# Attention's V projection made ahead of the scores: two tiles plainly, six in three pairs by Strassen's algorithm

## The chip, the cores and the metric

The kernel runs on one core of a Trainium2 chip. The metric is the device time of one execution in microseconds (us), lower is better. A core has a matrix engine (TensorE, PE in the profile), VectorE (DVE), ScalarE (ACT), GpSimd (POOL), a queue engine (SyncE, SP) and 16 DMA engines. Each engine works through its own instructions in the order in which the program has them, and waits on semaphores for the others. Matrix products are written to PSUM; the other tiles lie in SBUF. Only DVE, ACT and PE reach PSUM.

## The reference

Two pre-normed residual layers on x of 1024 x 1024, in float32. Layer one is a gated DeltaNet followed by a convolutional FFN, layer two is a banded softmax attention followed by another FFN. What the change touches is the way from the first FFN into attention:

```python
h = h + conv_ffn(rmsnorm(h, f_norm[0]), f_w_up[0], f_conv[0], f_conv_b[0], f_w_down[0])
kv = rmsnorm(h, kv_norm) @ w_kv            # K: columns 0..1023, V: columns 1024..2047
q = rmsnorm(h, b_norm) @ b_w_q
# for each of 16 heads of 64 and each chunk of 64 queries, a band of 9 chunks of keys
s = q_chunk @ k_band.T * 64 ** -0.5 + bias
o_chunk = softmax(s) @ v_band
h = h + o @ b_w_out
```

## The kernel before

**Numbers.** Every dense product in float32 is done as three products of reduced type: an operand is split into a high part (a cast on ACT, `xh`, `whi`, `uh`) and a low part (the difference, on POOL or DVE, `xl`, `wlo`, `ul`), and high x high, low x high and high x low are added up in one PSUM tile. Lines 118 to 120 hold the three matmuls of a plain tile (function `dense`), lines 1446 to 1448 those of the FFN.

**FFN 0.** Its up and down products go by Strassen's algorithm, with sums of weight blocks made by DVE, split by ACT and POOL (`r`, then `uh` and `ul`); the last tile of hidden columns is done plainly (`pul`, then the down products `pf`, with weights `fr` split into `fh` and `fl`). Everything around the end of the FFN stands in an order written out by hand: a list of steps for TensorE, and jobs hung at a step with a rank. SP issues the weight loads, POOL the accumulating stores `d_r<-stage`.

**Norm.** `norm_steps` (line 346 on) squares and sums h, and then makes, for each of the 8 row blocks k and for the half s of 512 tokens, `nt` (DVE), `xh` (ACT) and `xl` (line 381). With k even `xl` is made by DVE, with k odd by POOL.

**K0 and Q0.** `two_tiles` (line 1385) makes the K and the Q of the first pair of heads: first halves of both, with the rest of the norm's second half put in between, then second halves. Behind the second half of K0 the weights of V0 are loaded, folded with the norm's gain (line 98) and split (lines 101, 103).

**Attention.** There are 8 pairs of heads p. For each pair the kernel makes K, Q and V tiles of 128 columns, each in two halves of 8 x 3 matmuls (24 a half, 48 a tile). K and Q go through ACT and DVE (`kA`, `qA`, `qL`); V has to stand with tokens on partitions. For p = 0 that is done by transposes on TensorE (`pvt`); for p > 0 the tile is copied as 16-bit halves (`vt`), stored to DRAM (`d_vt`) and read back by a transposing DMA (`vu`), then joined (`vf`) and split into high and low (`V`). A score tile `sc` (lines 2293, 2294) is reduced and moved to `sS` by DVE (line 2298), raised by ACT (line 2302), divided by its sum by POOL (line 2308), transposed by TensorE (`ptp`, line 2353), split by ACT and DVE (`pTh`, `pTl`), and multiplied by V (`poT`, lines 2398, 2399), whose result ACT and DVE move to `oT`. There is one PSUM tile for `sc`.

**The order in attention** is made at build time by a planner (class `Flow`): it keeps an estimate of when DVE, ACT and POOL come free, emits score, transpose and apply groups when their inputs should be there, and otherwise matmuls of the next dense tile in its list `wv.dense`. That list holds for each pair K, Q and V (from p = 1 on; V from p = 0 on), in `queue_kv`. A K or Q tile may start when pair p - 2 is scored, a V tile when the outputs of pair p - 2 are done; their buffers come free then. After the last of them the tiles of the out-projection (`acco`) take their place.

Of the kernel before, what the change touches and what calls it, by code (L numbers as in the profile page):

```python
# [9 lines left out]
F32 = mybir.dt.float32  # L10
F32R = mybir.dt.float32r
# [7 lines left out]
KT = 8  # L19
# [9 lines left out]
def trunk_kernel(  # L29
# [1355 lines left out]
    def two_tiles(wts, tail, then):  # L1385

        pss = [[pacc.tile([P, HALF], F32, name="acc", tag="u", bufs=4) for _ in range(2)] for _ in wts]
        for s in range(2):
            for n, (ps, wt) in enumerate(zip(pss, wts)):
                for i in range(KT):  # L1390
                    dense(ps[s], wt, 0, xh, xl, FULL[i : i + 1], s, first=i == 0, last=i == KT - 1)
                    if (n, i) in ((0, 6), (1, 3)):
                        next(tail, None)
                if (s, n) == (1, 0):
                    then()
            for _ in tail:
                pass
            yield pss
# [8 lines left out]
    def ffn(layer, h, hp, xs, tail, d_r, last):  # L1407
# [475 lines left out]
        if layer == 0:  # L1883
# [187 lines left out]
        return right, norms[1] if norms else None  # L2071
# [8 lines left out]
    ctx_f, tail0 = ffn(0, h, hp, normed, tails[0], d_r0, xb)  # L2080
# [5 lines left out]
    def next_tile():  # L2086
        raw = wp.tile([P, KT, P], F32, name="wraw", tag="wraw", bufs=2)
        nc.sync.dma_start(out=raw, in_=w_kv[:, 1024 : 1024 + P].rearrange("(k p) m -> p k m", p=P))
        ready.append(split_w(raw, [P, KT, P], fold=g_kv))

    first = two_tiles([load_w(w_kv, 0, fold=g_kv, on_act=True), load_w(b_w_q, 0, fold=g_b, on_act=True)], tail0, next_tile)
    next(first)
# [4 lines left out]
    with ExitStack() as ph:  # L2097
# [21 lines left out]
        def kv_tile(src, c0, g, post):  # L2119

            if ready:
                wt = ready.pop()
                yield
            else:
                shape = [P, KT, P]
                raw = wp.tile(shape, F32, name="wraw", tag="wraw", bufs=2)
                nc.sync.dma_start(out=raw, in_=src[:, c0 : c0 + P].rearrange("(k p) m -> p k m", p=P))
                yield
                wt = split_w(raw, shape, fold=g)
                wv.on("G", 3.61, wv.on("A", 0.89, wv.on("G", 2.6)))  # L2130
# [13 lines left out]
        def queue_kv(p):  # L2144
# [18 lines left out]
            def post_q(s, ps):  # L2163
# [7 lines left out]
                def low():  # L2171
# [5 lines left out]
                    if s == 1:  # L2177
                        wv.mark(("kq", p), t)
# [545 lines left out]
```

## Time and profile before

| | us |
|---|---|
| median of 3 runs | 2497.43 (2497.12 to 2500.88) |
| span of the profiled execution | 2493.3 |
| DeltaNet and FFN 0, to the first K and Q matmul | 1295 |
| K0, Q0 and V0, to the first score | 37 |
| attention, first to last score (1332.4 to 1760.3) | 428 |
| the rest of the out-projection and FFN 1 | 733 |

Times in a row are from the span's start. In a timeline row the first number is the start, the second the duration; "x3" joins three like instructions; what stands in brackets is the idle time of the engine before the row and the engine and operation that ended it. In the rows of groups the total busy time and the mean of one in nanoseconds come after the bar. A matmul's duration in such a row covers its way through a pipeline, so that one starts well before the one ahead of it ends; what one costs TensorE is the interval between two starts.

### The profile page before, as it was taken

How to read it: one execution, taken by the hardware profiler on the slowest of the kernel's cores; microseconds unless marked ns; L12 is line 12 of the kernel's file. 1: busy time of each engine (PE TensorE's matmuls, PEld its weight loads, DVE VectorE, ACT ScalarE, POOL GpSimd, SP SyncE). 2: the span in 40 equal slices, each digit the busy share in tenths (PEclk: the TensorE clock that was granted, in tenths of full speed). 3: DMA queues.
4: the chain of work that ended last, by engine and by line, in shares of the span. 5: the costliest groups of instructions: out<-in, count | busy, mean ns of one | idle time of the engine just before them, and what ended most of it. 6: DMA issues, size and time to landing. Idle time of an engine off the chain costs nothing.

```text
span 2493.3 us, 39279 instructions
## 1 busy us (share of the span) xinstructions
PE 2466.1 (99%) x13785; PEld 2057.0 (83%) x13785; DVE 1842.5 (74%) x2985; ACT 1442.1 (58%) x2770; POOL 1523.0 (61%) x1548
## 2 busy tenths in 40 slices
PE   8999999999999999999999999999999999999998
PEld 6888888888888888888788888888877888888877
DVE  5665874567798888888866656666589788888886
ACT  6444546474465556565555666667456565666555
POOL 3655653357357777777626454455554777778774
PEclk9999999999999999999999999999999999999999
DMA  8734435565347777777841232333444799777788
GB/s 228 188 105 118 142 110 153 156 194 163 96 108 148 150 153 151 153 144 156 183 151 55 67 80 77 81 76 95 145 114 119 184 176 180 166 169 171 152 187 224
DMA packets 383877, 353.19 MB, mean 142 GB/s; under 512 B 97600, under 2 KB 304448, under 8 KB 383680
## 3 DMA queue, kind: packets, MB, share of 16 engines
q1 hardware_dynamic: 350704, 243.46, 34.4%
q0 software_dynamic: 28224, 98.58, 22.5%
q10 hardware_dynamic: 4752, 8.65, 0.9%
q8 instruction: 108, 1.77, 0.3%
q14 instruction: 89, 0.73, 0.1%
HBM read 182.25 MB, written 156.30 MB: 136 GB/s over the span
## 4 chain that ended last, share of the span: by engine, by line
PE 81%; POOL 6%; DVE 4%; issue 4%; DMA 2%; ACT 2%; SPq 0%; ACTq 0%; POOLq 0%; DVEq 0%
PE acc L118 8%; PE pu L1448 8%; PE acc L119 8%; PE acc L120 8%; PE pu L1446 8%; PE pu L1447 8%; PE pd L1448 3%; PE pd L1446 3%; PE pd L1447 3%; POOL ul L1412 3%; PE acco L118 2%; PE acco L120 2%; PE acco L119 2%; PE ptp L2353 2%; PE poT L2399 1%
## 5 line engine op out<-in xcount | busy, mean ns | idle before, releaser
L1412 POOL TENSOR_TENSOR ul<-r,uh 128x512 fp32r<-128x512 f32 x266 | 430.4, 1638 | 258.3 <-ACT uh L1434 253.5
L118 PE MATMUL acc<-xh,whi 128*128 128x512 f32 x896 | 369.3, 413 | 0.5 <-ACT xh L1094 0.5
L119 PE MATMUL acc<-xl,whi 128*128 128x512 f32 x896 | 352.1, 393 | 0.4 <-POOL xl L381 0.3
L120 PE MATMUL acc<-xh,wlo 128*128 128x512 f32 x896 | 351.3, 392 | 0.0
L103 POOL TENSOR_TENSOR wlo<-wraw,whi 128x256 fp32r<-128x256 f32 (+1 forms) x326 | 237.0, 758 | 107.8 <-ACT whi L101 105.3
L1434 ACT CAST uh<-r 128x512 fp32r<-128x512 f32 x289 | 177.1, 623 | 183.3 <-DVE r L1412 148.8
L1448 PE MATMUL pu<-xh,ul 128*128 128x512 f32 x524 | 204.4, 390 | 0.7 <-POOL ul L1412 0.7
L1446 PE MATMUL pu<-xh,uh 128*128 128x512 f32 x524 | 204.4, 390 | 0.7 <-ACT keep L1575 0.7
L1802 ACT COPY stage<-pd 128x1024 f32<-128x1024 f32 x180 | 175.3, 1014 | 49.7 <-PE pd L1448 48.8
L1447 PE MATMUL pu<-xl,uh 128*128 128x512 f32 x524 | 203.9, 389 | 0.0
L120 PEld LDWEIGHTS acc<-xh,wlo 128*128 128x128 f32 x896 | 168.5, 188 | 37.1
L2308 POOL TENSOR_SCALAR sS<-sS,st 128x640 f32<-128x640 f32 (+4 forms) x128 | 87.6, 691 | 178.4 <-DVE st L2306 168.2
L119 PEld LDWEIGHTS acc<-xl,whi 128*128 128x128 f32 x896 | 169.3, 189 | 28.4 <-POOL xl L381 2.5
L118 PEld LDWEIGHTS acc<-xh,whi 128*128 128x128 f32 x896 | 169.1, 189 | 27.5 <-ACT xh L1094 0.9
L1412 POOL TENSOR_TENSOR dl<-a,dh 128x512 fp32r<-128x512 f32 x90 | 153.3, 1703 | 47.4 <-ACT dh L1434 37.2
L1541 DVE SCALAR_TENSOR_TENSOR gate<-gpre,colt,gate 128x1023 f32<-128x1023 f32 (+2 forms) x92 | 176.5, 1919 | 2.5 <-ACT gate L1538 1.8
L1541 DVE SCALAR_TENSOR_TENSOR val<-vpre,colt,val 128x1023 f32<-128x1023 f32 x88 | 149.2, 1696 | 29.3 <-ACT val L1538 29.3
L2298 DVE CUSTOM_DVE_ANT_0 sS<-sc,bt 128x640 f32<-128x640 f32 (+4 forms) x128 | 84.1, 657 | 111.4 <-PE sc L2294 75.9
L1412 DVE TENSOR_TENSOR r<-r,r 128x512 f32<-128x512 f32 x160 | 130.3, 814 | 32.8 <-POOL ul L1412 31.7
L1412 DVE TENSOR_TENSOR el<-val,eh 128x512 fp32r<-128x512 f32 x90 | 85.4, 949 | 43.2 <-ACT eh L1434 43.2
L1448 PEld LDWEIGHTS pu<-xh,ul 128*128 128x128 f32 x524 | 98.4, 188 | 22.8 <-POOL ul L1412 1.4
L1446 PEld LDWEIGHTS pu<-xh,uh 128*128 128x128 f32 x524 | 98.4, 188 | 21.1 <-ACT keep L1575 1.1
(428 smaller groups left out, 7197.9 us busy)
## 6 DMA issues: line engine op xcount, KB each, us to landing
r<-in_f_w_up_dram SPq DMA_DIRECT2D x176, 256.0 KB, 4.5
d_r<-stage POOLq DMA_DIRECT2D x78, 512.0 KB, 8.1
d_c<-stage POOLq DMA_DIRECT2D x70, 512.0 KB, 8.4
a<-in_f_w_down_dram SPq DMA_DIRECT2D x72, 256.0 KB, 2.9
wraw<-in_a_w_in_dram SPq DMA_DIRECT2D x32, 512.0 KB, 4.5
d_e<-stage POOLq DMA_DIRECT2D x32, 512.0 KB, 8.3
wraw<-in_a_w_out_dram SPq DMA_DIRECT2D x16, 512.0 KB, 4.1
d_r<-h ACTq DMA_DIRECT2D x32, 256.0 KB, 2.8
```

The costliest lines, as they stand in the source:

```text
L103: nc.gpsimd.tensor_tensor(lo[:, c], raw[:, c], hi[:, c].bitcast(F32), op=ALU.subtract)
L118: mm(ps, hi[:, kw, wcol : wcol + P], rh[k][s], start=st, stop=False)
L119: mm(ps, hi[:, kw, wcol : wcol + P], rl[k][s], start=False, stop=False)
L120: mm(ps, lo[:, kw, wcol : wcol + P], rh[k][s], start=False, stop=sp)
L1412: tt = lambda eng, o, a, b, op: eng.tensor_tensor(o, a, b, op=op)
L1434: copy(hi, src)
L1446: mm(ps, w[0][:, cw], x[0], start=first, stop=False, skip_group_check=True)
L1447: mm(ps, w[0][:, cw], x[1], start=False, stop=False, skip_group_check=True)
L1448: mm(ps, w[1][:, cw], x[0], start=False, stop=last, skip_group_check=True)
L1541: nc.vector.scalar_tensor_tensor(t_[:, a:c1], p_[:, a - step : c1 - step], w[:, 2 - step : 3 - step], t_[:, a:c1], op0=ALU.mult, op1=ALU.add)
L1802: nc.scalar.copy(t_, ps)
L2308: nc.gpsimd.tensor_scalar(S, S, st[:, 3:4], 1.0, op0=ALU.mult, op1=ALU.mult)
```

## The change

- The eight V tiles are no longer made in attention. They are made between FFN 0 and the first score, in the pools of FFN 0, whose buffers stay open for that.
- V0 and V1 are made plainly: first halves in `first_halves`, which takes the place of `two_tiles` and carries the rest of the norm, second halves in the new `values`.
- V2 to V7 are made as three pairs. Pair j is a product of a weight block of 1024 x 256, taken as 2 x 2 blocks of 512 x 128 (`v11`, `v12`, `v21`, `v22`), with the normed activations as 2 x 2 blocks, by the seven products of Strassen's algorithm in Winograd's form. A product is 4 x 3 = 12 matmuls. Each needs a weight operand (a sum of blocks by DVE, `uh` by ACT, `ul` by POOL) and an activation operand (`X`: blocks of the norm's output, or sums that are made once for all three pairs and split).
- The raw weight blocks are loaded into buffers that FFN 0's last weights leave (tags `r11` to `r22` and the like), and folded with the gain on POOL.
- Every V half is copied to `vt` and stored to one of 16 `d_vt` tensors. In attention the transposing reads are all that is left of V; the `pvt` transposes go.
- Then K0 and Q0 are made in one go, just ahead of attention. `wv.dense` holds K and Q of pairs 1 to 7 only, 14 tiles in place of 22.
- The norm's second half is called with `keep=True`, which writes `nt` in place into h, and for which `norm_steps` has `xl` of k = 0..3 made by POOL and of k = 4..7 by DVE.

The core of the diff:

```diff
-    def two_tiles(wts, tail, then):
...
+    def first_halves(wts, tail):
+        pss = [pacc.tile([P, HALF], F32, name="acc", tag="u", bufs=4) for _ in wts]
+        for n, (ps, wt) in enumerate(zip(pss, wts)):
+            for i in range(KT):
+                dense(ps, wt, 0, xh, xl, FULL[i : i + 1], 0, first=i == 0, last=i == KT - 1)
+                if (n, i) in ((0, 6), (1, 3)):
+                    next(tail, None)
...
+    def values(wts, pss, raw, load, fh, fin, wf, wd, d_vt, more):
...
+        def lows(n, k):
+            tt(nc.gpsimd if k % 2 else nc.vector, X[n][k][1], place[n](k), X[n][k][0].bitcast(F32), sub)
+
+        def fold(j, q):
...
+            tt(nc.gpsimd, t_, t_, g, ALU.mult)
...
+        def operand(j, n):
+            left_sum(j, n)
+            src = raw[j, {1: 11, 2: 12, 7: 21, 6: 21, 5: 11, 4: 22, 3: 12}[n]]
+            hi, lo = ops[j, n] = [wf.tile([P, HALF], F32R, name="u" + x, tag="u" + x, bufs=3) for x in "hl"]
+            nc.scalar.copy(hi, src)
+            tt(nc.gpsimd, lo, src, hi.bitcast(F32), sub)
+
+        def product(j, n):
...
+            for k in range(4):
+                x_ = X[n][k]
+                mm(ps, wh[:, kc[k]], x_[0], start=o == n and k == 0, stop=False, skip_group_check=True)
+                mm(ps, wh[:, kc[k]], x_[1], start=False, stop=False, skip_group_check=True)
+                mm(ps, wl[:, kc[k]], x_[0], start=False, stop=k == 3, skip_group_check=True)
...
+        def out(tile_, s, src):
+            turn[0] ^= 1
+            vt = wf.tile([P, 2, 4, P], mybir.dt.uint16, name="vt", tag=("dh", "dl")[turn[0]], bufs=2)
+            nc.scalar.copy(vt.rearrange("p h b t -> p h (b t)"), src.bitcast(mybir.dt.uint16).rearrange("p (t h) -> p h t", h=2))
+            nc.sync.dma_start(out=d_vt[2 * tile_ + s].rearrange("(h b c) t -> c h b t", h=2, b=4), in_=vt)
...
+        plan = [(1, 1), (2, 1), (1, 2), (3, 1), (2, 2), (3, 2)] + [(j, n) for n in (7, 6) for j in range(1, 4)] + [(1, 5), (2, 5), (1, 3), (3, 5), (2, 3), (3, 3)] + [(j, 4) for j in range(1, 4)]
+        for j, n in plan:
+            step((j, n), lambda j=j, n=n: product(j, n))
+            at(pos[j, n] - 2, lambda j=j, n=n: operand(j, n), 1)
+            at(pos[j, n] + 1, lambda j=j, n=n: after(j, n), 0)
...
+        for j, i in ((1, -1), (2, 2), (3, 4)):
+            for q, d in ((11, 0), (12, 1), (21, 4), (22, 5)):
+                at(i + d, lambda j=j, q=q: fold(j, q), 0.5)
...
-                        norms.append(norm_steps(fh, s, None, last))
+                        norms.append(norm_steps(fh, s, None, last, keep=True))
...
-            for n, (src, c0, g, post) in enumerate(((w_kv, p * P, g_kv, post_k), (b_w_q, p * P, g_b, post_q), (w_kv, 1024 + p * P, g_kv, post_v))):
-                if p > 0 or n == 2:
-                    free = [] if p < 2 else [(("scored", "o")[n == 2], p - 2)]
-                    wv.dense.append((lambda: True, there(*free), kv_tile(src, c0, g, post)))
+            for src, g, post in ((w_kv, g_kv, post_k), (b_w_q, g_b, post_q)):
+                free = [] if p < 2 else [("scored", p - 2)]
+                wv.dense.append((lambda: True, there(*free), kv_tile(src, p * P, g, post)))
```

How the order of the instructions moves at three places. First POOL at the end of FFN 0, from the last but two `ul` of the last tile on. `fl` and `ul` are low parts of the down and up weights, `v11` and `v12` raw blocks of V's weights that are folded, and the `wlo` are the low parts of K0's and Q0's weights before, of V0's and V1's after. Before:

```order
L1412 TENSOR_TENSOR ul_12679<-r11_12494,uh_12678 128x512
L1412 TENSOR_TENSOR fl3_12708<-fr_12603,fh3_12707 128x512
L1412 TENSOR_TENSOR ul_12726<-r12_12608,uh_12725 128x512
L1412 TENSOR_TENSOR fl5_12836<-fr_12705,fh5_12835 128x512
L1412 TENSOR_TENSOR fl7_12844<-fr_12658,fh7_12843 128x512
```

After:

```order
L1564 TENSOR_TENSOR ul_12679<-r11_12494,uh_12678 128x512
L1400 TENSOR_TENSOR v11_13238<-v11_13238,colt_63 128x512
L1564 TENSOR_TENSOR fl3_12708<-fr_12603,fh3_12707 128x512
L1564 TENSOR_TENSOR ul_12726<-r12_12608,uh_12725 128x512
L1400 TENSOR_TENSOR v12_13240<-v12_13240,colt_63 128x512
L1564 TENSOR_TENSOR fl5_12836<-fr_12705,fh5_12835 128x512
L1564 TENSOR_TENSOR fl7_12844<-fr_12658,fh7_12843 128x512
L1400 TENSOR_TENSOR v11_13246<-v11_13246,colt_63 128x512
L103 TENSOR_TENSOR wlo_13221<-wraw_13210,whi_13220 128x1024
```

Two folds stand between low parts of the last tile, a third behind them.

Second POOL in the norm's second half and on from there. `xl1_1` is the low part of row block 1 in the second half of the tokens; `qL` are zeros put into attention's buffers. Before:

```order
L381 TENSOR_TENSOR xl1_1_13281<-nt_13314,xh1_1_13280 128x512
L381 TENSOR_TENSOR xl3_1_13285<-nt_13322,xh3_1_13284 128x512
L381 TENSOR_TENSOR xl5_1_13289<-nt_13330,xh5_1_13288 128x512
L381 TENSOR_TENSOR xl7_1_13293<-nt_13338,xh7_1_13292 128x512
L2112 MEMSET qL0_13444 64x1024
```

After:

```order
L381 TENSOR_TENSOR xl0_1_13309<-h0_12794,xh0_1_13308 128x512
L381 TENSOR_TENSOR xl1_1_13311<-h1_12795,xh1_1_13310 128x512
L381 TENSOR_TENSOR xl2_1_13313<-h2_12796,xh2_1_13312 128x512
L381 TENSOR_TENSOR xl3_1_13315<-h3_12797,xh3_1_13314 128x512
L1400 TENSOR_TENSOR ul_13423<-v11_13238,uh_13422 128x512
L1400 TENSOR_TENSOR v21_13242<-v21_13242,colt_63 128x512
L1400 TENSOR_TENSOR v12_13248<-v12_13248,colt_63 128x512
L1400 TENSOR_TENSOR ul_13450<-v11_13246,uh_13449 128x512
L1400 TENSOR_TENSOR xsum7_13383<-h1_12795,xsum7_13381 128x512
```

The blocks 0 to 3 stand in a row, and behind them the operands of V's products.

Third TensorE in attention, at the same score group in the middle of the phase (the 63rd of 128). `poT` is the product with V, `ptp` a transpose of probabilities, `sc` a score, `acc` a dense tile: the end of a Q tile in the first row of both. Before:

```order
L120 MATMUL acc_15888<-xh6_1_13290,wlo_15716 128x512
L2398 MATMUL poT_15962<-pTh_15948,V_15433 128x128
L2399 MATMUL poT_15962<-pTl_15949,V_15433 128x128
L2398 MATMUL poT_15962<-pTh_15948,V_15433 128x128
L2399 MATMUL poT_15962<-pTl_15949,V_15433 128x128
L2353 MATMUL ptp_16009<-ident_65,sS_15832 128x128
L2353 MATMUL ptp_16009<-ident_65,sS_15863 128x128
L2353 MATMUL ptp_16009<-ident_65,sS_15832 128x128
L2353 MATMUL ptp_16009<-ident_65,sS_15863 128x128
L2293 MATMUL sc_16019<-kA_15035,qA_15207 128x320
L2294 MATMUL sc_16019<-kA_15035,qL1_13849 128x320
```

After:

```order
L120 MATMUL acc_16337<-xh7_1_13322,wlo_16043 128x512
L2550 MATMUL poT_16384<-pTh_16368,V_15555 128x128
L2551 MATMUL poT_16384<-pTl_16369,V_15555 128x128
L2550 MATMUL poT_16384<-pTh_16368,V_15555 128x128
L2551 MATMUL poT_16384<-pTl_16369,V_15555 128x128
L2505 MATMUL ptp_16430<-ident_65,sS_16265 128x128
L2505 MATMUL ptp_16430<-ident_65,sS_16332 128x128
L2505 MATMUL ptp_16430<-ident_65,sS_16265 128x128
L2505 MATMUL ptp_16430<-ident_65,sS_16332 128x128
L2445 MATMUL sc_16443<-kA_15415,qA_15716 128x320
L2446 MATMUL sc_16443<-kA_15415,qL1_14393 128x320
```

The rows read alike; what differs is what follows. Before, five instructions further on, six matmuls of `acc` come in (the last of this Q tile and the first of a V tile), and six more after another twelve. After, 29 instructions run from the row behind `acc_16337` to the next dense matmul, `acc_16504`, the first of the next pair's K tile.

More of the change, by code (lines that the diff above doesn't have):

```diff
@@ L2083, in trunk_kernel @@
     xh, xl = xb
-    ready = []
[L2086 to L2092, printed above, removed]
+    U16 = mybir.dt.uint16
+    d_vt = [dram.tile([2 * HALF, P], U16, name=f"d_vt{i}") for i in range(16)]
@@ L2139, in kv_tile @@
                 yield
-        U16 = mybir.dt.uint16
-        d_vt = [dram.tile([2 * HALF, P], U16, name=f"d_vt{i}") for i in range(4)]
         def queue_kv(p):
```

235 lines of the change are left out of this document (168 added, 67 removed).

## The prediction

> **What bounds the kernel now.** I read the page's first two sections, then the waits of TensorE, then windows by stage.
>
> ```profile
> span 2493.3 us, 39279 instructions
> PE 2466.1 (99%) x13785; PEld 2057.0 (83%) x13785; DVE 1842.5 (74%) x2985; ACT 1442.1 (58%) x2770; POOL 1523.0 (61%) x1548
> ```
>
> The profiled span is 2493.3 us; the median of the runs, 2497.4, is 4.1 us above it. I take these 4.1 us as lying around the span and work from 2497.4. TensorE is busy for 99% of the span, so work taken from it is worth its issue time, if nothing else becomes late. What is late now, in TensorE's waits:
>
> ```profile
> PE ptp L2353 <- DVE pTl L2373: 0.8, 5, 0.2
> PE acc L119 <- POOL xl L381: 0.3, 1, 0.3
> ```
>
> The columns are the total, the count and the longest. Attention (scores to outputs) shows 0.8 us of waits in all. The same, as a window from the first score to the last:
>
> ```profile
> 1332.40:1760.30 427.90, 427.08 (x2501) 375.86 (x2500) 271.17 (x735) 281.20 (x652) 215.44 (x340) 1.00 0.30 79
> ```
>
> The columns are the length, then the busy time of PE, weight loads, DVE, ACT and POOL, the granted clock, the DMA share and GB/s. DVE is busy for 63% of attention and ACT for 66%. Their work hides beside TensorE's, because much of what TensorE does there is dense filler:
>
> ```profile
> L118 PE MATMUL acc<-xh,whi 128*128 128x512 f32 x336 | 134.7, 401 | 0.0
> L119 PE MATMUL acc<-xl,whi 128*128 128x512 f32 x337 | 132.0, 392 | 0.0
> L120 PE MATMUL acc<-xh,wlo 128*128 128x512 f32 x337 | 131.6, 390 | 0.0
> ```
>
> That is 1010 matmuls of the K, Q and V tiles, and 105 more of the out-projection (`acco`) in the same window. Their means overlap; the interval from one to the next is read from the timeline:
>
> ```profile
> 1245.09 0.39 PE L1448 MATMUL pul<-xh,ul 128*128 128x512 f32 x1
> 1245.32 0.40 PE L1446 MATMUL pul<-xh,uh 128*128 128x512 f32 x1
> ```
>
> It is 0.23 us. So 1115 dense matmuls take 256 us of attention's 427, and the other 1386 instructions share 171 us, 0.124 us each.
>
> **The work that goes.** Eight V tiles take 8 x 48 = 384 matmuls; after, two plain tiles take 96 and 21 products of 12 take 252. 36 matmuls fewer at 0.23 are 8.3 us. The eight `pvt` transposes go too: 0.8 us at some 0.1. **Term: -9.1.**
>
> **The end of FFN0.** The first listing shows POOL's order here; the trace of before has it so:
>
> ```profile
> 1231.97 1.62 POOL L1412 TENSOR_TENSOR ul<-r,uh 128x512 fp32r<-128x512 f32 x1
> 1233.23 1.59 POOL L1412 TENSOR_TENSOR fl<-fr,fh 128x512 fp32r<-128x512 f32 x1
> 1234.47 1.60 POOL L1412 TENSOR_TENSOR ul<-r,uh 128x512 fp32r<-128x512 f32 x1
> 1237.51 1.41 POOL L1412 TENSOR_TENSOR fl<-fr,fh 128x512 fp32r<-128x512 f32 x1 [1.44 <-ACT fh L1874]
> 1242.93 1.82 POOL L1412 TENSOR_TENSOR ul<-r,uh 128x512 fp32r<-128x512 f32 x1 [4.02 <-ACT uh L1434]
> ```
>
> The last `ul` ends at 1244.75, and TensorE uses it at 1245.09: 0.34 us to spare. The fold of `v11` now stands ahead of the last `fl` and that `ul`, and waits for its load. SP issues that load behind the last `fr`:
>
> ```profile
> 1233.62 5.38 SPq L1863 DMA_DIRECT2D fr<-in_f_w_down_dram  x3
> r<-in_f_w_up_dram SPq DMA_DIRECT2D x176, 256.0 KB, 4.5
> d_r<-stage POOLq DMA_DIRECT2D x78, 512.0 KB, 8.1
> ```
>
> Issue at some 1239.4, landing 4.5 later at 1243.9; the fold by the nearest row (`fl`) 1.4, then `fl` 1.4 and `ul` 1.8: 1248.5, which is 3.4 us after TensorE's need. The DMA engines are near full here, with more loads added:
>
> ```profile
> 1200.00:1250.00 50.00, 49.87 (x219) 40.62 (x218) 41.94 (x36) 26.27 (x36) 31.89 (x26) 1.00 0.91 202
> ```
>
> So I take 4. The ends: 0, if the load is out early and POOL's idle 4.02 us covers it, and 8, if it lands as late as `d_r` does (8.1 against 4.5). **Term: +4.** The `wlo` of V0 and V1 stand behind two more such folds; the last tile's down products, which TensorE works through before it starts on V, cover that.
>
> **The norm's second half.** The four `xl` of k = 0..3 now run one after the other on POOL (second listing), where DVE did every other one. TensorE takes one k in three matmuls, 0.69 us.
>
> ```profile
> 1306.86 1.89 DVE L390 TENSOR_TENSOR nt<-psb,h 128x512 f32<-128x512 f32 x3 [2.75 <-PE psb L385]
> 1309.20 0.62 PE L118 MATMUL acc<-xh,whi 128*128 128x512 f32 x2
> 1308.89 1.62 POOL L381 TENSOR_TENSOR xl<-nt,xh 128x512 fp32r<-128x512 f32 x1 [3.62 <-ACT xh L393]
> 1310.68 1.53 POOL L381 TENSOR_TENSOR xl<-nt,xh 128x512 fp32r<-128x512 f32 x1 [0.18 <-ACT xh L393]
> ```
>
> With the first `xl` possible at some 1308.2 (0.6 for `nt`, 0.6 for `xh`) and 1.3 to 1.6 us each, k = 3 is ready at 1313.4 to 1314.6; TensorE, which starts this half at 1309.2, wants it at 1311.5. That is 1.9 to 3.1, less the 0.3 that the waits row shows for `xl` already. **Term: +2** (ends 1 and 3).
>
> **Products of V.** TensorE has 48 + 252 matmuls, 69 us. POOL has 4 `xl`, 21 `ul`, 9 folds and 8 low parts of operand sums, 42 operations of 128x512, and 8 `wlo` pieces of 128x256:
>
> ```profile
> L1412 POOL TENSOR_TENSOR ul<-r,uh 128x512 fp32r<-128x512 f32 x266 | 430.4, 1638 | 258.3 <-ACT uh L1434 253.5
> L103 POOL TENSOR_TENSOR wlo<-wraw,whi 128x256 fp32r<-128x256 f32 (+1 forms) x326 | 237.0, 758 | 107.8 <-ACT whi L101 105.3
> ```
>
> At these means: 42 x 1.638 + 8 x 0.758 = 75 us; at the 1.26 us between the starts at 1231.97 and 1233.23, 59. POOL is late by 0 to 6 us; each left operand is made two products ahead, which smooths little. The means were taken with DVE beside it, as here. **Term: +2.5.**
>
> **Attention without V as filler.** 7 of the 21 tiles leave the window: 336 x 0.23 = 77 us of cover. The saving is counted above; here is what it uncovers. K and Q of pair p may only start when pair p-2 is scored, so the 14 tiles left are used up within each pair. In the order before, the longest run of score, transpose and apply instructions without a dense matmul has 24 rows. After, one has 70, one 66, one 33, three have 29, and the last, where only out-projection is left, 82 (third listing: a run's start, against the same scores before).
>
> DVE's work in a run is priced by these rows:
>
> ```profile
> L2298 DVE CUSTOM_DVE_ANT_0 sS<-sc,bt 128x640 f32<-128x640 f32 x63 | 51.8, 823 | 49.9 <-PE sc L2294 36.8 <-POOL sS L2308 12.4 <-POOL wlo L103 0.3
> L2373 DVE TENSOR_TENSOR pTl<-ptp,pTh 128x512 fp32r<-128x512 f32 x75 | 50.4, 685 | 6.6 <-ACT pTh L2366 5.7
> L2409 DVE TENSOR_TENSOR oT<-poT,tm 64x256 f32<-64x256 f32 x60 | 25.6, 427 | 3.3 <-ACT tm L2404 1.6
> L2373 DVE TENSOR_TENSOR pTl<-ptp,pTh 128x256 fp32r<-128x256 f32 x61 | 25.0, 419 | 4.2 <-ACT pTh L2366 4.0
> L2306 DVE RECIPROCAL st<-st 128x1 f32<-128x1 f32 x126 | 19.8, 158 | 7.4 <-ACT sS L2302 5.8
> L2173 DVE SCALAR_TENSOR_TENSOR qL<-acc,qA 64x512 fp32r<-64x512 f32 x28 | 19.2, 687 | 12.4 <-ACT qA L2169 12.2
> L2175 DVE CAST qA<-qA 64x512 fp32r<-64x512 f32 x28 | 12.1, 433 | 0.4
> L2298 DVE DVE_READ_ACCUMULATOR2_ANT st<- 128x1 f32 x127 | 10.6, 83 | 0.0
> L2373 DVE TENSOR_TENSOR pTl<-ptp,pTh 128x128 fp32r<-128x128 f32 x32 | 9.0, 281 | 0.0
> ```
>
> A run of 29 has 2 score reductions with their reads (1.8), 1 + 2 + 2 `pTl` (2.1), 3 reciprocals (0.5), 2 `qL` and 2 `qA` copies (2.2) and 2 `oT` (0.9): 7.5 us. DVE's groups in the window add up to 299 us where it was busy for 271, since rows overlap at their ends: x 0.9, 6.7. TensorE's 29 rows take 29 x 0.124 = 3.6. Excess 3.1. In the same way: 33 rows, 7.8 against 4.1, 3.7; 66 rows, 11.0 against 8.2, 2.8; 70 rows, 11.3 against 8.7, 2.6; 82 rows, 10.9 against 10.2, 0.7. Sum 3 x 3.1 + 9.8 = 19. How far DVE is ahead when a run begins covers part of it: before's 20 runs of 20 to 24 rows have an excess of up to 0.5 us each and pass almost without a wait, so I take off 0.5 for each of the seven. **Term: +16.** Why a wait cannot slip to later: scores have one PSUM tile, so the next score waits for the reduction, and that stands behind `qL` and `qA` on DVE, which wait for the Q tile that ended just ahead. The ends: 3, if planning ahead hides nearly all, and 27 (no lead, rows not scaled).
>
> Nothing else comes near: the 16 DMA transposes of V stand behind 16 stores, and attention's DMA share is 0.30; the out-projection is the same.
>
> **Sum.** 2497.4 - 9.1 + 4 + 2 + 2.5 + 16 = **2512.8 us**.
>
> **The rivals.**
> *Filler isn't missed* (faster). With attention's waits at 3 and FFN0's at 0 or 1, the rest being the low ends (norm 1, products 0), -9.1 + 4.5 gives 2493; with none in attention 2490. For it: DVE and ACT, at 271 and 281 of 350 us, stay under TensorE's load on average, and the planner sees their backlog. Against: runs three times as long as any before. The point from which it decides is 9.1 us of waits in all.
> *Break-even*: attention 6, FFN0 2 and norm 2 give 2498.
> *POOL bounds the products* (slower still). If every operation takes the 1.79 us between the two `xl` above, POOL needs 42 x 1.79 + 6 = 81 us against 69: 12 late in place of 2.5, 2522. The Trainium skill (GPSIMD Engine Reference, 8. Key points) says that GpSimd shares its SBUF interfaces with VectorE and suffers beside DVE instructions with two SBUF inputs, and DVE has some 35 of those here; the spread of 1.26 to 1.79 agrees with it, without showing the cause.
> *TensorE's clock falls* after long waits. The trace has one, at the start:
>
> ```profile
> 7.05 0.88 PE L1181 MATMUL pxt<-ident,xt 128*128 128x128 f32 x3 [7.05 <-DVE xt L1091]
> 12.15 0.79 PE L118 MATMUL acc<-xh,whi 128*128 128x512 f32 x1 [0.45 <-ACT xh L1094]
> 15.24 0.63 PE L119 MATMUL acc<-xl,whi 128*128 128x512 f32 x1
> 15.66 0.63 PE L120 MATMUL acc<-xh,wlo 128*128 128x512 f32 x1
> 17.00 0.40 PE L119 MATMUL acc<-xl,whi 128*128 128x512 f32 x1
> 17.23 0.39 PE L120 MATMUL acc<-xh,wlo 128*128 128x512 f32 x1
> ```
>
> After 7.05 us without work an interval is 0.42 at 15.24, and 0.23 again at 17.00. One such fall costs some 2.4 us (half of 12.15 to 17.00); at seven runs and FFN0's stall, 19 more: 2532. Against: my waits come in pieces below 3.1 us. The Trainium skill (TensorE: Matmul & The Clock Gate, What's actually happening) puts the idle window that halves the clock at about 3.4 us; the start agrees, and no shorter wait in this trace tests it.
>
> **Chances.** Forecast 0.53 (own range 2503 to 2521), POOL-bound 0.07, clock 0.04; break-even 0.17; faster 0.19. Below 0.2%, 5 us, a measurement of this kernel can't tell a change from none. So faster 0.19, same 0.17, slower 0.64. The range leaves out about half of the faster case and the two dearest: 2491 to 2525.
>
> **What would show it.** Waits of TensorE for DVE or ACT at `sc`, `ptp` and `poT` of 12 us or more in attention, in seven clusters, once a pair where Q has ended; 3 to 5 us at the last `pul` product behind a POOL fold; 2 us at V0's second half; few waits among `pv`. It is wrong if attention's window comes to 351 us (427 - 77) with its waits below 5, or if the products take over 75 us.

## The result and the profile after

The changed kernel takes **2558.8 us** (median of 4 runs, 2555.01 to 2561.97) against 2497.44 before (2497.12 to 2500.88): ratio 1.0246, 95% interval 1.0231 to 1.026. It is slower, as forecast, but by 61 us where 15 were forecast, and far outside the range.

First the page of the profile after and TensorE's waits (total, count, longest):

```profile
span 2560.3 us, 39405 instructions
PE 2488.0 (97%) x13741; PEld 2064.4 (81%) x13741; DVE 1885.7 (74%) x3036; ACT 1466.9 (57%) x2824; POOL 1550.6 (61%) x1533
...
PE sc L2445 <- DVE st L2450: 16.4, 15, 2.7
...
PE pv L1477 <- POOL ul L1400: 7.6, 6, 5.6
PE pul L1600 <- POOL ul L1564: 6.8, 2, 5.6
PE poT L2550 <- DVE oT L2561: 2.9, 4, 1.7
PE acco L119 <- POOL xl L2601: 2.4, 1, 2.4
PE ptp L2505 <- DVE pTl L2525: 2.3, 3, 1.6
PE pm L862 <- issue: 2.3, 1, 2.3
...
PE acc L119 <- POOL xl L381: 1.6, 4, 0.7
```

TensorE has 44 matmuls fewer (36 products and 8 transposes, as counted in the forecast) and yet is busy 22 us longer. That is the first sign of something that no list of waits can show: some of the same instructions took longer. The two windows of the part that was rebuilt, V with K0 and Q0, and attention (length, busy time of PE, weight loads, DVE, ACT and POOL, granted clock, DMA share, GB/s):

```profile
1311.00:1431.30 120.30, 110.94 (x470) 87.36 (x469) 66.13 (x86) 60.07 (x101) 83.48 (x68) 0.97 0.28 63
1431.30:1819.90 388.60, 364.10 (x2139) 318.55 (x2139) 275.35 (x739) 261.83 (x633) 180.34 (x283) 0.97 0.25 70
```

The granted clock was 1.00 in attention before and is 0.97 now. The profile's record of the granted clock has it at 0.50 in eight stretches before the end of the program: from 533.2 (6.8 us long), 1256.9 (6.8), 1342.2 (6.8), 1516.3 (3.4), 1570.9 (6.8), 1622.1 (3.4), 1669.9 (6.8) and 1721.1 (3.4). Before the change that record, which begins at 16.6, has none ahead of the last matmuls. Each costs at most half its length, and less where TensorE still waits when the clock falls: 22 us at most, of which 12 in attention.

The stages side by side, each from TensorE's first matmul of one kind to that of the next (us):

| stage | before | after | difference | forecast |
|---|---|---|---|---|
| DeltaNet, to FFN 0's first product | 643.2 | 649.6 | +6.4 | 0 |
| FFN 0, to its last tile | 584.3 | 585.5 | +1.2 | 0 |
| FFN 0's last tile, to `pf` | 22.5 | 30.5 | +8.0 | +4 |
| `pf`, to the first V (before: K) matmul | 45.4 | 45.4 | 0 | 0 |
| V, K0, Q0, to the first score | 37.1 | 120.3 | +83.2 | } |
| attention, first to last score | 427.6 | 388.6 | -39.0 | } +11.4 together |
| rest of the out-projection | 72.6 | 74.1 | +1.5 | 0 |
| FFN 1 and the end | 660.4 | 666.2 | +5.8 | 0 |

The two rebuilt stages together gained 44.2 us where 11.4 were forecast. Worked out from counts and the interval of 0.23 us: attention lost 346 dense matmuls (1010 to 664), 79.6 us, so it lost 39.0 only because 40.6 were added, of which waits are 23.4 (24.2 now, 0.8 before) and half rate 11 to 12; some 6 are in neither. The V stage gained 309 dense matmuls less the transposes, 70.3 us, and 12.9 more: waits 9.2 (`pv` 7.6, `acc` 1.6), half rate at most 2.4, and a rest.

**FFN 0's end.** The chain of work that ended last, followed back from TensorE's late product (start, duration, what):

```profile
1242.03 1.25 POOL ul L1564
1243.29 0.08 SPq L2244
...
1243.46 5.35 SPq L2015
...
1248.90 5.05 DMA v<-in_w_kv_dram
...
1254.11 0.07 POOL v L1400
1254.17 0.93 issue
1255.11 1.26 POOL fl L1564
1256.37 1.23 POOL ul L1564
1257.60 0.04 issue
1257.64 0.80 PE pul L1600
1258.44 0.43 PE pul L1598
```

The load `v` stands on SP behind a load of `fr` whose issue was held for 5.35 us; it lands at 1253.95, and fold, `fl` and `ul` follow one another on POOL, in the order that the first listing had. TensorE waited 5.6 us there. The two last rows show the second price: an interval of 0.43 us where the same matmuls took 0.23.

**Attention.** The cluster of the third listing, where Q of a pair has ended, is shown here on TensorE and, behind "...", on DVE:

```profile
1568.18 0.31 PE L2446 MATMUL sc<-kA,qL 128*128 128x320 f32 x1
1568.33 0.49 PE L2505 MATMUL ptp<-ident,sS 128*128 128x128 f32 x3
1571.52 0.63 PE L2445 MATMUL sc<-kA,qA 128*128 128x320 f32 x1 [2.71 <-DVE st L2450]
...
1566.74 0.83 DVE L2450 CUSTOM_DVE_ANT_0 sS<-sc,bt 128x640 f32<-128x640 f32 x1 [1.56 <-PE sc L2446]
1567.49 1.39 DVE L2356 SCALAR_TENSOR_TENSOR qL<-acc,qA 64x512 fp32r<-64x512 f32 x2
1568.89 0.86 DVE L2358 CAST qA<-qA 64x512 fp32r<-64x512 f32 x2
1569.78 0.17 DVE L2458 RECIPROCAL st<-st 128x1 f32<-128x1 f32 x1
1569.86 0.74 DVE L2386 TENSOR_TENSOR V<-vf,V 128x256 fp32r<-128x256 f32 x2
1570.64 0.82 DVE L2450 CUSTOM_DVE_ANT_0 sS<-sc,bt 128x640 f32<-128x640 f32 x1
```

A score is ready for reduction at 1568.5 and is reduced only at 1570.64, behind `qL`, `qA` and V's low part. The wait is 2.7 us, and it comes back at 1621.56, 1670.55 and 1720.78 with 2.68 each. What follows such a wait shows in four windows of 3.41 us:

```profile
1567.48:1570.90 3.42, 1.18 (x7) 0.93 (x7) 3.32 (x10) 3.40 (x10) 0.79 (x1) 1.00 0.00 0
1570.90:1574.31 3.41, 2.79 (x13) 2.69 (x13) 3.26 (x11) 1.29 (x4) 1.38 (x5) 0.50 0.00 0
1574.31:1577.72 3.41, 3.41 (x16) 3.12 (x14) 1.49 (x6) 1.78 (x5) 1.88 (x3) 0.50 0.55 162
1577.72:1581.14 3.42, 3.42 (x22) 3.04 (x21) 2.08 (x6) 1.72 (x5) 0.00 (x0) 1.00 0.31 90
```

In the first, TensorE was busy for 1.18 us of 3.42 at full clock; the next two have the clock at 0.50, the fourth is at 1.00 again. So behind a wait of 2.7 us the clock stood at half for 6.8 us, in the first 0.6 of which TensorE still waited: up to 3.1 us on top of the 2.7.

**V's products.** POOL made one `ul` in 8.59 us (its group's mean is 1.76), while DVE made the sums of the activations. POOL first, DVE behind "...":

```profile
1335.57 8.59 POOL L1400 TENSOR_TENSOR ul<-v,uh 128x512 fp32r<-128x512 f32 x1 [6.33 <-ACT uh L1461]
...
1335.73 2.48 DVE L1400 TENSOR_TENSOR h<-h,h 128x512 f32<-128x512 f32 x4
...
1338.74 2.48 DVE L1400 TENSOR_TENSOR h<-h,h 128x512 f32<-128x512 f32 x4
1341.15 1.88 DVE L1400 TENSOR_TENSOR xsum<-h,xsum 128x512 fp32r<-128x512 f32 x3
```

TensorE's `pv` waited 5.56 us for this one, of the 7.6 in all, until 1344.2. The clock stood at half from 1342.2 to 1349.0, so at most 2.4 us were lost to it behind the wait.

### The profile page after: what moved, and what is told of

The parts are those of the page before. It is cut to its first block, busy times and chain, and to the rows that moved or that the text cites. A ratio compares the mean times of both kernels' runs of the same rounds, so it can differ in the third digit from the quotient of the medians.

```text
span 2560.3 us, 39405 instructions
## 1 busy us (share of the span) xinstructions
PE 2488.0 (97%) x13741; PEld 2064.4 (81%) x13741; DVE 1885.7 (74%) x3036; ACT 1466.9 (57%) x2824; POOL 1550.6 (61%) x1533
## 3 DMA queue, kind: packets, MB, share of 16 engines
q0 software_dynamic: 28224, 98.58, 21.8%
## 4 chain that ended last, share of the span: by engine, by line
PE 72%; POOL 7%; DVE 6%; issue 5%; DMA 5%; ACT 2%; SPq 1%; ACTq 0%; POOLq 0%; DVEq 0%
PE pu L1600 7%; PE acc L118 7%; PE acc L119 7%; PE pu L1598 7%; PE pu L1599 7%; PE acc L120 6%; POOL ul L1564 3%; PE pd L1598 3%; PE pd L1600 3%; PE pd L1599 3%; DMA d_rt<-rm 2%; PE acco L118 2%; PE acco L120 2%; PE acco L119 2%; PE ptp L2505 2%
## 5 line engine op out<-in xcount | busy, mean ns | idle before, releaser
L118 PE MATMUL acc<-xh,whi 128*128 128x512 f32 x800 | 333.6, 417 | 0.4 <-ACT xh L1094 0.4
L119 PE MATMUL acc<-xl,whi 128*128 128x512 f32 x800 | 316.2, 395 | 1.7 <-POOL xl L381 1.6
L120 PE MATMUL acc<-xh,wlo 128*128 128x512 f32 x800 | 315.3, 394 | 0.0
L103 POOL TENSOR_TENSOR wlo<-wraw,whi 128x256 fp32r<-128x256 f32 (+1 forms) x294 | 216.1, 766 | 99.3 <-ACT whi L101 97.9
L1693 DVE SCALAR_TENSOR_TENSOR gate<-gpre,colt,gate 128x1023 f32<-128x1023 f32 (+2 forms) x92 | 173.4, 1885 | 11.4 <-ACT gate L1690 10.7
L120 PEld LDWEIGHTS acc<-xh,wlo 128*128 128x128 f32 x800 | 151.4, 189 | 33.4
L119 PEld LDWEIGHTS acc<-xl,whi 128*128 128x128 f32 x800 | 152.4, 191 | 27.0 <-POOL xl L381 4.1
L118 PEld LDWEIGHTS acc<-xh,whi 128*128 128x128 f32 x800 | 152.2, 190 | 24.1 <-ACT xh L1094 0.8
```

The lines of the kernel that those rows point to most:

```text
L103: nc.gpsimd.tensor_tensor(lo[:, c], raw[:, c], hi[:, c].bitcast(F32), op=ALU.subtract)
L118: mm(ps, hi[:, kw, wcol : wcol + P], rh[k][s], start=st, stop=False)
L119: mm(ps, hi[:, kw, wcol : wcol + P], rl[k][s], start=False, stop=False)
L120: mm(ps, lo[:, kw, wcol : wcol + P], rh[k][s], start=False, stop=sp)
L1693: nc.vector.scalar_tensor_tensor(t_[:, a:c1], p_[:, a - step : c1 - step], w[:, 2 - step : 3 - step], t_[:, a:c1], op0=ALU.mult, op1=ALU.add)
```

## The experiments

The kernel before took 2498.3 to 2498.5 us beside these runs, and each run has a profile. Parts are compared stage by stage, since the stop in DeltaNet (the `pm` row above) comes and goes between executions; the repeat of the unchanged kernel, told first, shows it.

**The changed kernel once more** (e12_after_again), with no edit.

> The changed kernel once more. In the trace of after TensorE stops in DeltaNet at 531 us for 2.3 us without waiting for anything that the profile shows, and its clock falls afterwards; the code there is the one of before. If it comes from chance in the execution, the stop may be missing or have another length now, and DeltaNet up to FFN 0's first product takes 643 us as before in place of 649.6. If it comes from the program, it is there again at the same matmul with 2 to 3 us.

Measured: 2552.7 us, ratio 1.0216 (1.0195 to 1.0236). DeltaNet took 644.4 us in place of 649.6, with no stop at `pm` and no half rate there. V took 120.4 and attention 387.7, as in the first profile. So some 5 us of the 61 come and go with the same program. Whether the change plays a part in them is not shown: of the eleven profiles of the changed kernel and its variants nine have a stop of 0.6 us or more there, the one profile of before has none. The repeat as a whole is some 54 us slower than the kernel before (2552.7 - 2498.5). Attention's half-rate stretches came again, at 1561.0 (6.8 us), 1612.2, 1663.4 and 1711.2 (3.4 each), not quite as many.

**FFN 0's end: fold behind the last tile** (e1_fold_late). The fold reads the gain from a copy that POOL makes behind the last `fl` and `ul`, and so cannot come ahead of them.

```diff
+    g_v = rowt[:, 0:8]
...
-            g = g_kv[:, k0 : k0 + 4].rearrange("p (k o) -> p k o", o=1).broadcast_to([P, 4, P])
+            g = g_v[:, k0 : k0 + 4].rearrange("p (k o) -> p k o", o=1).broadcast_to([P, 4, P])
...
+            at(pos["f", 0, 0], lambda: nc.gpsimd.tensor_copy(g_v, g_kv), 5)
```

> The folds of V's weights are held until POOL has made the last low parts of FFN 0 (they read their gain from a copy that POOL makes there). Theory (a fold that waits for its load holds up the last ul): the wait of 5.6 us at the last pul product goes, and with it the fall of the clock at 1256.9 (6.8 us at half rate, 3.4 us lost): about 9 us less than the changed kernel, near 2549. Rival (the load of the last up weight itself comes late, being behind V's loads on SP): the wait stays at 4 us or more and the time within 2 us of the changed kernel.

Measured: 2551.37 us, 1.0205 (1.019 to 1.022). The last tile took 22.4 us in place of 30.5 (22.5 before), the half rate behind it is gone, and the V stage stayed at 120.4. The whole +8.0 was the fold's place on POOL.

**Low part of Q later** (e2_low_later). The planner is told that `qL` and `qA` come free later, so that DVE gets to the score first.

```diff
-                wv.later(wv.on("A", 0.30), low)
+                wv.later(wv.on("A", 0.30) + (2.0 if s == 1 and 0 < p < 7 else 0.0), low)
```

> The low parts and copies of Q's second half (qL, qA on DVE) are queued 2 us later for pairs 1 to 6, so that the reduction of the pair's last score should stand ahead of them. Theory (the wait of 2.7 us in the middle of the long runs is the reduction standing behind qL and qA): the four to five waits of 2.7 us at sc fall under 1.2 us and most of the five half-rate stretches in attention go: 12 to 20 us less. Rival (DVE has too much work in these stretches, whatever its order): the waits move to the next score, the sum of waits in attention stays above 20 us, and the time stays within 5 us.

Measured: 2557.9 us, 1.0234 (1.0218 to 1.0249); attention 386.5 against 388.6. TensorE's waits in this kernel:

```profile
PE poT L2550 <- DVE oT L2561: 8.5, 7, 2.7
...
PE ptp L2505 <- DVE pTl L2525: 6.2, 7, 2.9
PE sc L2445 <- DVE st L2450: 5.0, 9, 0.9
```

The wait at `sc` went from 16.4 to 5.0 and came up at `poT` and `ptp`; all waits in attention come to 24.2 again, as the rival said. Which DVE instruction stands first doesn't matter; DVE has more to do in the run than TensorE has without dense matmuls.

**TensorE kept busy in the wait** (e3_warm). In pairs 1 to 5, eight matmuls whose result is not used are put into the long run; 40 in all, 9.2 us of added work.

```diff
+            full = None
+            if 0 < u[1] < 6 and u[2:] == (1, 3, 1):
+                full = pacc.tile([P, HALF], F32, name="warm", tag="acc", bufs=3)
+                for j in range(8):
+                    mm(full, kA[a][:, 0:P], kA[a][:, 0:HALF], start=j == 0, stop=j == 7)
```

> Eight matmuls of 128x512 with a result that nothing uses are put ahead of the score that waits 2.7 us, for pairs 1 to 5; they take 1.84 us each time, inside the wait. Theory (TensorE's clock falls after such a wait): the waits shrink to about 0.9 us, the half-rate stretches after them (3.4 or 6.8 us, 24 us in attention) go, and the kernel gains up to 12 us although it does 40 matmuls more. Rival (the half-rate stretches cost nothing, since DVE is what sets the pace there): the time stays within 3 us of the changed kernel, or rises by up to 9 if the matmuls don't fit into the waits.

Measured: 2545.85 us, 1.0192 (1.0177 to 1.0207), without the stop in DeltaNet. Attention took 383.7 us against 388.6 although TensorE had 40 matmuls more. The largest of its waits in attention:

```profile
PE sc L2450 <- DVE st L2455: 8.1, 13, 1.2
```

The waits at `sc` are half of what they were, and none is longer than 1.2; half rate in attention went from 23.9 us to 3.4, the one stretch left coming behind `acco`'s wait of 2.4 us. Added work 9.2, waits less by 6.6 (24.2 to 17.6), half rate less by 10.2: 7.6 less, of which 4.9 was measured. The half rate is the only thing seen that can have made the stage shorter than the added work and the waits allow, by 7.5 us (9.2 - 6.6 + 4.9). So waits of 2.7 us let the clock fall, and that costs time of its own.

**The filler put back** (e4_dummy_v). A third dense tile of 48 matmuls is put behind Q for pairs 1 to 6, copied and stored like a V tile and not used.

```diff
+            if p < 7:
+                wv.dense.append((lambda: True, there(*([("o", p - 2)] if p > 1 else [])), kv_tile(w_kv, 1024 + p * P, g_kv, post_none)))
```

> For pairs 1 to 6 a dense tile of 48 matmuls with V's weights is put back into attention's list behind Q (copied and stored, its result unused); V itself is made in front as in the changed kernel. TensorE has 288 matmuls more, 66 us. Theory (filler is what attention lacks): the waits in attention fall from 24 us to under 6, the half-rate stretches go, and the time rises by only 66 - 18 - 12 = 36 us or less, near 2590. Rival (V's way through DRAM, or the order of the scores, makes the waits): the waits stay at 20 us or more, and the time rises by 60 us or more, to 2618 and above.

Measured: 2589.76 us, 1.0371 (1.0354 to 1.0388). The longest run without dense work fell to 23 rows. 288 matmuls are 66 us of TensorE's time, and attention grew by 39.8 (428.4 against 388.6): 26 us of them took no time. Waits fell by 16.5, to 7.7 us, and no half rate is left in the six pairs (one stretch of 3.4 us, at 1809.9, behind the last), up to 10 us less; together that makes the 26:

```profile
PE sc L2454 <- DVE st L2459: 2.1, 2, 1.5
```

So missing filler, and not another property of the changed attention, made its waits.

**Sums of the activations later** (e5_sums_late). The jobs that make the sums and their high and low parts are moved back, so that they don't run beside POOL's first `ul`. In the trace two of the four groups did move.

```diff
-        for f, n, i in ((sums, 7, 0), (highs, 7, 0), (sums, 6, 1), (highs, 6, 2), (sums, 5, 3), (sums, 4, 4), (highs, 5, 9), (highs, 4, 13)):
+        for f, n, i in ((sums, 7, 4), (highs, 7, 4), (sums, 6, 6), (highs, 6, 7), (sums, 5, 9), (sums, 4, 10), (highs, 5, 11), (highs, 4, 14)):
...
-        for n, i in ((7, 3), (6, 6), (5, 10), (4, 14)):
+        for n, i in ((7, 6), (6, 9), (5, 12), (4, 16)):
```

> The sums of activation blocks for products 7, 6, 5 and 4 (16 DVE operations with two inputs in SBUF, which DVE does almost in one row of 12 us as the products begin) are put 4 to 6 products later, each still ahead of its use. Theory (POOL cannot get at its operands while DVE does such operations without a pause: its first ul took 8.59 us instead of 1.3 to 1.7): the first ul takes under 3 us, the wait of 5.6 us at pv and the half-rate stretch at 1342 go, 6 to 9 us less than the changed kernel. Rival (the first ul waits for its data, or is slow by itself): it keeps taking 6 us or more, and the time stays within 2 us.

Measured: 2553.22 us, 1.0223 (1.0207 to 1.024). The same `ul`, and TensorE's waits for `ul`, in this kernel:

```profile
1330.05 2.55 POOL L1400 TENSOR_TENSOR ul<-v,uh 128x512 fp32r<-128x512 f32 x1 [5.17 <-ACT uh L1461]
...
PE pv L1477 <- POOL ul L1400: 5.4, 8, 1.8
```

8.59 us became 2.55: the long `ul` came from its neighbours on DVE. The half rate at 1342 went as well. But the V stage went only from 120.3 to 118.4, not the 6 to 9 us less of the forecast: the waits came back in smaller pieces (5.4 at `ul`, 1.0 at ACT's `uh`, 1.6 at `xl`, 8.0 in all against 9.2). Its matmuls alone would make the stage 107.4 us (37.1 + 70.3); 3.0 of the 11.0 above that are in no wait, at full clock, where the changed kernel has 3.7. So the half rate cost hardly 1 us here.

**Dense work paced** (e8_pace). A dense step of pair p may not go out before a number of scores that grows with the step, and K may start earlier, so that the 14 tiles are spread over each pair.

```diff
-                        yield
+                        yield lambda q=16 * (p - 1) - 3 + 0.5 * (n0 + 8 * s + i + 1): nsc[0] >= q
...
-                free = [] if p < 2 else [("scored", p - 2)]
...
+                free = [] if p < 2 else [("sc", p - 2, 1, 2) if post is post_k else ("scored", p - 2)]
```

> Attention's 14 dense tiles are spread: a matmul triple of pair p may come only after half as many scores of the pair before (two triples a score), and K's first half may start three scores before the buffers of pair p-2 are free, its result moved after. The longest run of instructions without a dense matmul falls from 70 to 23, but for the last pair (74). Theory (attention waits because filler comes bunched, while on the average it suffices: DVE 271 us and ACT 267 of some 351): the waits in attention fall from 24 us to under 10 and the half-rate stretches to one at most: 20 to 28 us less than the changed kernel, attention's window near 362 us. Rival (filler is too little on the whole, however it is spread): the waits stay above 18 us, spread over many scores, attention's window stays above 378 us.

Measured: 2539.33 us, 1.016 (1.0143 to 1.0176). The longest run fell to 23 rows, except for the last pair's. Attention took 371.9 us against 388.6 with no half rate in it. Its waits stayed at 18 us in all:

```profile
PE ptp L2509 <- DVE pTl L2529: 12.3, 7, 3.3
...
PE sc L2448 <- DVE st L2453: 3.5, 5, 1.1
```

Of the 26.6 us that the forecast took off the window 16.7 came: the half rate went, and a quarter of the waits. The waits stayed above 18 us, as the rival said, but the window came far below its 378. Seven waits at `ptp` are left, 1.8 us each on average; the next run shows one. This run also checks the price of half rate. The counts give 348.0 us for attention (427.6 - 79.6), waits 17.5 more than before, and 6.4 are left with no half rate at all. The changed kernel has 40.6 - 23.4 = 17.2 beyond its waits; less the same 6.4 that is 10.8, close to half of its 23.9 us at half rate.

**All mends together** (e9_all): the late fold, the late sums, the paced dense work, and `xl` of the norm's second half again alternating between DVE and POOL.

```diff
-            eng = (nc.gpsimd if k in (0, 1, 2, 3) else nc.vector) if keep and s == 1 else (nc.vector if k % 2 == 0 else nc.gpsimd)
+            eng = nc.vector if k % 2 == 0 else nc.gpsimd
```

> The late folds, the late sums, the spread filler, and the norm's low parts again alternating between DVE and POOL, together. If the parts add up: FFN 0's end 9 less, products 9, norm 1.5, attention 24: 2515 us, by which the kernel still loses to the one before. If they get into each other's way, above 2525.

Measured: 2529.38 us, 1.0128 (1.0111 to 1.0145). The last tile 21.8 us, V 118.6, attention 372.3: each stage has what its own mend gave it alone, so the mends don't get into each other's way. The 2515 was missed because the parts are smaller than was put in: V gave 1.7 us in place of 9, attention 16.3 in place of 24. One of the waits left in attention, on TensorE and, behind "...", on DVE:

```profile
1553.39 0.52 PE L2511 MATMUL ptp<-ident,sS 128*128 128x128 f32 x3 [1.71 <-DVE pTl L2531]
...
1549.53 1.39 DVE L2360 SCALAR_TENSOR_TENSOR qL<-acc,qA 64x512 fp32r<-64x512 f32 x2 [0.61 <-ACT qA L2356]
1550.93 0.86 DVE L2362 CAST qA<-qA 64x512 fp32r<-64x512 f32 x2
```

Again it is `qL` and `qA`, 2.25 us on DVE ahead of what TensorE needs.

**Folds on ACT** (e10_folds_act): e9, and the folds taken from POOL.

```diff
-            tt(nc.gpsimd, t_, t_, g, ALU.mult)
+            for c in range(4):
+                nc.scalar.activation(t_[:, c], t_[:, c], AF.Copy, scale=g_v[:, k0 + c : k0 + c + 1])
```

> As e9_all, with the folds of V's Strassen weights (9 during the products, 1.04 us or more each) made by ACT in four pieces of 128x128 in place of POOL. Theory (POOL sets the pace of the products, so that a wait taken away in one place comes back in another): POOL loses 9 to 13 us of its work there, the waits for POOL at pv fall from 5.5 us to under 2, the stretch from the first V matmul to the first score falls from 118.6 us to 111 to 114. Rival (the order of the operands, not POOL's load, makes the waits): the stretch stays above 117 us.

Measured: 2526.25 us, 1.0117 (1.0091 to 1.0144). The V stage fell from 118.6 to 116.2. TensorE's wait for `ul`, in e9 and then here:

```profile
PE pv L1478 <- POOL ul L1401: 5.5, 7, 1.8
```

```profile
PE pv L1478 <- POOL ul L1401: 1.7, 4, 0.6
```

POOL's load made this wait, but only a quarter of its folds' 10 us came back, and 116.2 lies between the theory's 111 to 114 and the rival's 117. The stage is still 8.8 us above 107.4; some 6 of them are waits, these 1.7, 1.6 for `xl` and 2.7 for `uh` and the copies of the products, which ACT now makes later.

**Copies of Q on POOL as well** (e11_light): e10, with `qA` copied by POOL in place of DVE.

```diff
-                        nc.vector.tensor_copy(qA[a][r2, c], qA[a][r, c].bitcast(F32))
+                        nc.gpsimd.tensor_copy(qA[a][r2, c], qA[a][r, c].bitcast(F32))
```

> As e10_folds_act, and the copies of Q's high part to the other half of the partitions (28 in attention, 0.43 us each) made by POOL in place of DVE. Theory (a wait once a pair stands behind qL and qA on DVE): each chain is 0.86 us shorter; the six waits of 1.8 us or so at ptp fall below 1.2 us, attention's window falls from 372 us to 364 to 368. Rival (POOL, which needs more time for a copy and shares access with DVE, delays the next pair's first score): the window stays at 371 us or grows.

Measured: 2527.8 us, 1.012 (1.0103 to 1.0137); as a whole no different from e10. In its profile attention took 367.4 us against 372.8, as the theory said (364 to 368), so a lighter DVE in the run is worth 5 us there. Its waits are shorter one by one, and most of their sum is still there:

```profile
PE ptp L2511 <- DVE pTl L2531: 10.2, 12, 3.1
```

No version beats the kernel before.

## Why the prediction was right in its sign and wrong in its size

- **The work that goes (-9.1): the count right.** It is 44 matmuls fewer. The 9.1 us can't be seen by themselves; the balance above uses the same 0.23 us each.
- **FFN 0's end (+4): the mechanism right, the term mis-sized.** It measured +8.0, and e1 gives all of it back. The step "Issue at some 1239.4, landing 4.5 later at 1243.9" failed: the whole program stood some 7.6 us later by then, which makes that 1247.0, and the load went out at 1248.90, 1.9 later, because another load's issue was held ahead of it on SP; it landed in 5.05. The wait was 5.6 us where 3.4 were worked out. The other 2.4 are put down to the half rate that followed, which can have cost up to 3.0.
- **The norm's second half (+2): about right.** Waits for `xl` 1.6 us.
- **Products of V (+2.5): too low, though POOL had no more work than was counted.** The waits at `pv` are 7.6 us. POOL was busy for 83.5 us in the stage, but 18 of its operations there are none that the forecast counted; the 50 that it did count took 70.0, inside its 59 to 75. What it missed is one of them: a single `ul` of 8.59 us at the start, beside DVE's sums, when the left operands are only two ahead. The mean spread over the stage hid that. One sign of being wrong came true: "if the products take over 75 us"; from V0's second half at 1324.69 to the end of the last product at 1408.45 they took 83.8. The rival "POOL bounds the products" (12 us late, chance 0.07) came near the stage's 12.9 by luck, since its mechanism, every operation at 1.79 us, did not happen (and 0.18 of its 1.79 is idle time of that row).
- **Attention without filler (+16): right in kind and place, too small.** A run of 29 was priced at 3.1 less 0.5; the wait once a pair is 2.7 (four of them at 2.68 to 2.71). They came at `sc`, behind `qL` and `qA` on DVE, as the forecast said. All waits came to 24.2 us against the 16.8 that the term means (16, and 0.8 from before): the four repeating waits are 10.7, about their price, but the run of 70 has 4.5 where 2.1 were left to it, that of 82 has 2.5 where 0.2 were, and 2.4 at `acco` were not foreseen. e4 shows that the filler was the cause, and e2 that the order of DVE's work was not.
- **The step that failed: "Against: my waits come in pieces below 3.1 us."** With it the rival "TensorE's clock falls" was given 0.04 and nothing in the sum, since the only fall in the trace of before stood behind 7.05 us. The clock fell, and behind waits of 1.6 to 5.6 us: for 23.9 us in attention, which cost some 11, and behind the two stalls ahead, which cost about 2.4 at FFN 0's end and hardly 1 at V. The rival had 19 us, eight falls at 2.4, where these come to some 14. e3 took the waits' length and the half rate away together with matmuls that do nothing, and the stage became shorter for it.
- **What the terms missed.** They measured -9.1 + 8.0 + 12.9 + 40.6 = 52.4 in the first profile (the repeat as a whole is 54 us slower than before) where the forecast had 15.4. Of the 37 us between them some 13 are half rate, some 14 are waits priced too low (7.4 in attention, 4.7 in the V stage, 1.6 at FFN 0's end), and some 10 are in neither.
- **What was not foreseen:** DeltaNet's +6.4. The code there is that of before, and e12 shows the same kernel with +1.2. FFN 1 and the end took 660.0 to 670.8 us over these profiles with the same code, so +5.8 there is not read as an effect either.
- **Still open:** the 10 us that by this count are in no wait and at full clock, some 6 in attention and 3 to 4 in the V stage.

## What to carry to other kernels

Dense matmuls that stand between dependent groups are cover: taking 80 us of them out of attention shortened it by 39 only; the rest came back as waits, as half rate and as time in neither. Price a wait on TensorE at more than its length: one that left TensorE idle for over 2 us of a 3.4 us window was followed here by 3.4 or 6.8 us at half rate, up to 1.7 or 3.4 us lost. So a few long waits can cost more than many short ones, and pacing the dense work pays even where most of the waits stay. A load whose consumer stands ahead of urgent work on an in-order engine makes that work wait for the queue ahead of the load as well.

## What the runs showed of the hardware

**The clock.** All half-rate stretches of a run start at whole multiples of 3.413 us from one another (1256.9 and 1342.2 are 25 windows apart, 1570.9 and 1622.1 are 15), and last one or two such windows. Over the eleven profiles of the changed kernel and its variants, with a window's idle time taken as its length less TensorE's busy time in it: all 32 windows at full clock with 2.1 us or more of idle time were followed by a fall; of those with 1.6 to 2.1, 10 of 37; below 1.6 only five were, the lowest with 1.42. So a wait's place on the grid matters beside its length. `acco`'s wait, just ahead of 1773.26, lies across two windows and let nothing fall; both rows have the clock at 1.00:

```profile
1768.86:1772.28 3.42, 1.98 (x11) 1.32 (x9) 3.35 (x8) 3.04 (x7) 2.93 (x5) 1.00 0.21 78
1772.28:1775.69 3.41, 2.44 (x12) 2.13 (x13) 3.35 (x6) 1.63 (x5) 3.41 (x3) 1.00 0.34 92
```

The Trainium skill (TensorE: Matmul & The Clock Gate, What's actually happening) speaks of an idle window of about 3.4 us; the window's length agrees with the 3.413 here, but it need not be idle throughout: 1.18 us of work in 3.42 did not keep the clock. Where the two differ, these rows decide.

**POOL beside DVE.** The same `ul` took 8.59 us beside DVE's sums, in each of the seven profiles that have them there, and 2.55 when most of them had moved away (e5), while DVE went on at 0.62 us an operation. In both cases it ended 1.1 us behind the end of DVE's unbroken row of operations (1343.03 and, in e5, 1331.45), little less than the 1.27 that the quickest `ul` takes in all: it got next to nothing done until DVE paused. The price can fall on DVE instead: in e5 four of the moved sums, from 1345.42 on, took 6.59 us beside POOL's operations, where four took 2.48 before. The Trainium skill (GPSIMD Engine Reference, 8. Key points) says that GpSimd shares its SBUF interfaces with VectorE and contends with DVE instructions that have two inputs in SBUF; the trace agrees, and puts the price at some 6 us for one operation.

**A stop in DeltaNet.** At one and the same matmul of `pm` TensorE stood still with no semaphore to wait for, 0.6 to 3.1 us in nine of the eleven profiles of the changed kernel and its variants, less than 0.1 in e3, and not at all in the repeat or before. In six of them 3.4 or 6.8 us at half rate followed. The page's line of the DMA queue that loads instructions (packets, MB, share) and, behind "...", TensorE's row behind the stop:

```profile
q8 instruction: 108, 1.77, 0.3%
...
533.55 0.26 PE L862 MATMUL pm<-T,mn 32*32 32x32 f32 x2 [2.29 <-issue]
```

The queue brings 16 KB a packet. One of its packets is under way from 531.21 to 532.16 here, and TensorE goes on at 533.55; in e5, with the longest stop, from 531.14 to 532.10, and TensorE goes on at 533.47. In all ten profiles with a stop TensorE goes on 1.2 to 1.5 us after that packet has landed; in the repeat it landed at 529.90, ahead of the matmul. By these times TensorE waited for its own instructions. Why the packet comes late in some executions the runs do not show.
